# HGRN2 mixer without zero-padded queries: products over a head's 64 rows, results on that parity's partitions, scores and state part in one accumulator

## The chip, the core and the metric

The kernel runs on one core of a Trainium2 chip. The core has five engines that run side by side, each with its own instruction queue, executed in order: TensorE (PE in the rows; its weight loads are shown as PEld), VectorE (DVE), ScalarE (ACT), GpSimd (POOL) and SyncE (SP, which only starts transfers here). An engine waits for another through semaphores. The metric is the device time of one execution in microseconds (us).

## What is computed

One inference step of a two-layer decoder trunk, 512 prompt tokens and 8 single-token samples, 1024 features. Each layer normalises its input, projects it with one matrix, hands the columns to four mixers (A: HGRN2, B: RWKV-7, C: dilated attention, D: pooling), gates them, and projects back. The change is in mixer A, which has 4 heads of 64 features and runs in chunks of 64 tokens:

```python
def step(s, inp):                       # one chunk; q, k, v, log f per head
    G = jnp.cumsum(gb, axis=2)
    o_inter = jnp.einsum('bhtk,bhkv->bhtv', qb * jnp.exp(G), s)
    diff = G[:, :, :, None, :] - G[:, :, None, :, :]
    decay = jnp.where(causal, jnp.exp(jnp.where(causal, diff, 0.0)), 0.0)
    att = jnp.einsum('bhtk,bhsk,bhtsk->bhts', qb, kb, decay)
    o_intra = jnp.einsum('bhts,bhsv->bhtv', att, vb)
    s_new = exp(G_last) * s + einsum('bhsk,bhsv->bhkv', kb * exp(G_last - G), vb)
    return s_new, o_inter + o_intra
```

## The kernel before

Activations lie with features on the 128 partitions and tokens along the free dimension. The 256 features of mixer A are two tiles `th` of 128; each tile holds two heads, one on partitions 0 to 63 and one on 64 to 127 (their parity, `pp`; `ROWS` are the two slices).

The input projection (`project`, tiles `pj`) is the bulk of TensorE's work: every operand is split in two exact parts (`hh`, `hl` for the input, `whi`, `wlo` for the weights; POOL makes `wlo`, ACT `whi`), and three matmuls of 256 or 264 columns are made per product. The class `Flow` writes TensorE's program in one order: it takes steps of the mixers' generators (`stream_A`, `stream_B`, ...), whose `yield cost, latency` says how long a step is thought to keep TensorE and how long the next one has to wait for other engines, and lays steps of the projections between them. A scheduler then moves instructions within limits. Since each engine runs in order, a TensorE instruction that waits for DVE holds up every projection behind it.

`stream_A` per layer: the queries `aq` are copied into `aqz`, which has for each chunk and head the query in that head's 64 rows and zeros in the other 64 (two tiles, one per `th`). `adg` holds products of keys and queries of the same token (the diagonal of the scores `aatt`). `sample_values` and the loop behind it handle the 8 samples. `to_tokens` turns the values by transposes on TensorE (`tok`, then `avtm`, 128 tokens on the partitions). Then six levels follow, for blocks of 1, 2, ..., 32 tokens: at each, `alv` holds the products of the keys in the left halves with the queries in the right halves of every pair of blocks, DVE writes them into the scores where a mask says so (line 727), and queries, keys and the block decays (`atot`) are scaled for the next level (lines 731 to 739); the queries of parity 0 on DVE, those of parity 1 on POOL. Behind the levels come the samples' read (`srd`), the keys turned (`aktm`), the state products of all chunks (`akv`), the states `aS` by a chain on DVE, and the outputs: `ao` within the chunks and `aos` from the states before them, in two PSUM tiles, added by DVE.

In `alv` a matmul has the 64 keys of a chunk over all 128 rows as its stationary operand and both heads' padded queries as 64 columns:

```python
mm(p[ROWS[c % 2], x:x + 64].rearrange("p (a n b) -> p a n b", a=2, b=b),
   k[:, th, 64 * c:64 * c + 64],
   qz[th][:, c].rearrange("p a (n w b) -> p a n w b", w=2, b=b)[:, :, :, 1, :])
```

A matmul with fp32 operands stands in the trace as two records. The size in a record (`128*64`) is the rows and columns of the stationary operand; a result on partitions 0 to 63 or 64 to 127 uses the left or right half of the array's columns, operands on one half of the partitions use one half of its rows. `stream_B` runs beside A; in this text its tiles `sBt`, `sBa` (samples' state), `bZ`, `bA`, `bMB` (products of a chunk), `bT` (an inverse by substitution on DVE), `bX`, `bXT`, `bU`, `bS` appear.

## Time and profile before

| | |
|---|---|
| median of 3 runs | 782.69 us (782.3 to 784.27) |
| profiled execution, first to last instruction (span) | 781.0 us |
| TensorE busy | 715.5 us (92%) |
| VectorE busy | 593.2 us (76%) |
| GpSimd busy | 384.7 us (49%) |
| ScalarE busy | 365.2 us (47%) |

The profile tells of the profiled execution only its span; the median of the runs lies 1.7 us above it. Busy time is the union of an engine's instructions. TensorE's records overlap and their ends are modelled, so its share tells where it waits rather than how fast it works.

### The profile page before, as it was taken

The page shows a single profiled execution, that of the slowest core. Times are in us where ns is not written, and L with a number is a line of the kernel's source. Part 1 is how long each engine was busy: PE and PEld are TensorE (multiplying, and loading weights), DVE is VectorE, ACT ScalarE, POOL GpSimd, SP SyncE. Part 2 cuts the span into 40 slices and gives each one's busy share as a digit, 9 for nine tenths or more (in the row PEclk, how much of TensorE's full clock was granted, in tenths as well). Part 3 has the DMA queues.
Part 4 walks back from the last instruction along what each step waited for, and adds up shares of the span by engine and source line. Part 5 has one row for each costly group of instructions (what it writes and reads, how often), then busy time and mean ns, then how long its engine had stood idle before and what let it go on. Part 6 is the DMA issues. An engine that isn't in the chain of part 4 may idle for free. (4 is left out here: it accounts for less than half of the span.)

```text
span 781.0 us, 18348 instructions
## 1 busy us (share of the span) xinstructions
PE 715.5 (92%) x7297; PEld 626.3 (80%) x7297; DVE 593.2 (76%) x1263; ACT 365.2 (47%) x778; POOL 384.7 (49%) x348
## 2 busy tenths in 40 slices
PE   2999989698789999999998999879889999999998
PEld 1687769487779998787888989768778989777898
DVE  4558759999998465788747897986999765587873
ACT  5233667014243465674235688412233547477520
POOL 2335427874753243236637756686554332223662
PEclk9999999897899999999998999899889999999999
DMA  9979755152232155337263323515232134135222
GB/s 330 351 276 335 226 168 153 41 163 69 82 98 56 40 183 192 125 97 272 69 190 96 118 68 98 147 56 150 69 95 86 56 99 150 56 113 163 98 77 102
DMA packets 67446, 105.74 MB, mean 135 GB/s; under 512 B 18336, under 2 KB 26848, under 8 KB 67360
## 3 DMA queue, kind: packets, MB, share of 16 engines
q1 hardware_dynamic: 67216, 104.50, 41.8%
q8 instruction: 57, 0.93, 0.5%
q14 instruction: 29, 0.24, 0.1%
q10 hardware_dynamic: 144, 0.06, 0.0%
HBM read 88.20 MB, written 14.22 MB: 131 GB/s over the span
## 5 line engine op out<-in xcount | busy, mean ns | idle before, releaser
L237 POOL TENSOR_TENSOR wlo<-wraw,whi 128x512 fp32r<-128x512 f32 x144 | 203.1, 1416 | 235.4 <-ACT whi L261 203.8
L269 PE MATMUL pj<-hh,whi 128*128 128x256 f32 (+1 forms) x928 | 278.0, 308 | 17.9 <-DVE raw L632 6.9
L269 PE MATMUL pj<-hl,whi 128*128 128x256 f32 (+1 forms) x928 | 268.3, 296 | 0.6 <-DVE hl L254 0.6
L269 PE MATMUL pj<-hh,wlo 128*128 128x264 f32 (+1 forms) x896 | 262.2, 298 | 0.5 <-POOL wlo L237 0.5
L269 PEld LDWEIGHTS pj<-hh,whi 128*128 128x128 f32 x928 | 182.3, 200 | 36.1 <-issue 12.6
L269 PEld LDWEIGHTS pj<-hl,whi 128*128 128x128 f32 x928 | 183.1, 200 | 4.6 <-issue 2.7
L269 PEld LDWEIGHTS pj<-hh,wlo 128*128 128x128 f32 x896 | 176.3, 199 | 6.2 <-issue 4.1
L261 ACT ACTIVATE whi<-wraw 128x512 fp32r<-128x512 f32 (+1 forms) x146 | 90.6, 623 | 161.5 <-PE pj L269 128.6
L269 PE MATMUL pj<-ml,whi 128*128 128x264 f32 (+1 forms) x256 | 72.5, 286 | 2.0 <-DVE cst L250 1.4
L269 PE MATMUL pj<-mh,whi 128*128 128x256 f32 (+1 forms) x256 | 72.6, 291 | 0.3 <-ACT mh L261 0.3
L269 PE MATMUL pj<-mh,wlo 128*128 128x256 f32 (+1 forms) x256 | 71.5, 283 | 0.0
L237 POOL TENSOR_TENSOR gate<-gate,raw 128x520 f32<-128x520 f32 x16 | 22.1, 1383 | 69.9 <-ACT gate L258 34.3
L254 DVE SCALAR_TENSOR_TENSOR x<-pj,mod,x 128x256 f32<-128x256 f32 x64 | 30.8, 481 | 33.1 <-PE pj L269 32.7
L269 PEld LDWEIGHTS pj<-mh,whi 128*128 128x128 f32 x256 | 47.4, 188 | 4.8 <-issue 2.6
L269 PEld LDWEIGHTS pj<-ml,whi 128*128 128x128 f32 x256 | 48.2, 188 | 3.3 <-DVE ml L237 2.7
L269 PEld LDWEIGHTS pj<-mh,wlo 128*128 128x128 f32 x256 | 48.0, 188 | 0.6 <-POOL wlo L237 0.4
L269 PE MATMUL ada<-adaw,sc 128*32 128x256 f32 (+1 forms) x448 | 33.9, 375 | 11.9 <-DVE nacc L237 11.8
L269 PEld LDWEIGHTS ada<-adaw,sc 128*32 128x32 f32 x448 | 12.4, 115 | 20.6 <-DVE nacc L237 11.8
L269 PE MATMUL alv<-aqz,ak 128*64 128x64 f32 x384 | 20.6, 249 | 6.6 <-DVE ak L237 6.6
L254 DVE SCALAR_TENSOR_TENSOR bX<-bX,bfac,bS 64x64 f32<-64x64 f32 x56 | 15.6, 279 | 14.2 <-PE bS L269 12.8
L269 PEld LDWEIGHTS alv<-aqz,ak 128*64 128x64 f32 x384 | 17.2, 157 | 10.0 <-issue 4.5
L1123 DVE COPY bUV<-bU 64x128 f32<-64x128 f32 x16 | 4.7, 295 | 23.3 <-ACT bUV L261 23.1
(409 smaller groups left out, 1456.1 us busy)
## 6 DMA issues: line engine op xcount, KB each, us to landing
wraw<-in_w_in_dram SPq DMA_DIRECT2D x112, 256.0 KB, 2.8
adaw<-in_ada_w_dram SPq DMA_DIRECT2D x48, 512.0 KB, 5.5
wraw<-in_w_out_dram SPq DMA_DIRECT2D x32, 256.0 KB, 2.8
x<-in_x_dram SPq DMA_DIRECT2D x8, 520.0 KB, 5.8
ckT<-in_ckT_dram SPq DMA_DIRECT2D x8, 320.0 KB, 3.2
x<-xmid SPq DMA_DIRECT2D x4, 520.0 KB, 5.8
cvr<-in_cvr_dram SPq DMA_DIRECT2D x4, 512.0 KB, 5.3
xmid<-x SPq DMA_DIRECT2D x7, 260.0 KB, 2.0
```

The lines of the kernel that those rows point to most:

```text
L237: return eng.tensor_tensor(out=out, in0=a, in1=b, op=op)
L254: return V.scalar_tensor_tensor(out=out, in0=a, scalar=s, in1=b, op0=op0, op1=op1)
L261: return A.activation(out, a, AF.Copy)
L269: return PE.matmul(out, lhsT, rhs, start=start, stop=stop)
L1123: V.tensor_copy(UV[ROWS[1], 1], pv[ROWS[1]])
```

## The change

The padded queries are gone: `aq` itself is scaled in place, and every product of mixer A takes one head's 64 rows on both sides, with the result on the same 64 partitions. `to_rows` takes the place of `to_tokens` for keys and values (a product with a piece of the identity instead of a transpose). A level makes 32 matmuls of 32 columns instead of 16 of 64, and the masked copy into the scores stands behind the scaling for the next level. The scaling of the queries is done on DVE over 128 partitions, POOL has none of it. Scores and state part go into one accumulator, so the copies and sums behind `ao` become one copy per half. The costs and latencies in the `yield`s are other numbers too. Comments are removed throughout, which moves line numbers by two at most outside `stream_A`.

```diff
@@ -660,39 +660,49 @@
             ts(k, k, omlb[:, l, j:j + 1], ALU.mult)
         return use
 
+    def to_rows(dst, src):
+
+        for hf in range(2):
+            p = mm_ps("rows")
+            for c in range(4 * hf, 4 * hf + 4):
+                for th in range(2):
+                    i = 64 * (2 * (c % 4) + th)
+                    for pp, r in enumerate(ROWS):
+                        mm(p[r, i:i + 64], src[r, th, 64 * c:64 * c + 64], ident[r, 64 * pp:64 * pp + 64])
+            copy(dst[:, 8 * hf:8 * hf + 8, :], p.rearrange("p (i d) -> p i d", d=64))
+            yield 800.0, 700.0 * hf
+
     def stream_A(l, L, flow):
+
         yield "aq1"
         yield 0.0, 3500.0
         q = L.t["aq"]
         att = f1k("aatt").rearrange("p (a t) -> p a t", t=64)
-        # each chunk's queries, per head with zeros in the other head's rows
-        qz = [f1k("aqz").rearrange("p (c a t) -> p c a t", a=2, t=64) for _ in range(2)]
-        for th in range(2):
-            G.memset(qz[th], 0.0)
-            for pp, r in enumerate(ROWS):
-                copy(qz[th][r, :, pp, :], q[r, th, PR].rearrange("p (c t) -> p c t", t=64))
         zq = sample_queries(q[:, :, SM])
-        yield 0.0, 2500.0
+        yield 0.0, 1000.0
         yield "af1"
         f, k = L.t["af"], L.t["ak"]
+
+        def chunk(x, r, c, th):
+            return x[r, th, 64 * c:64 * c + 64]
 
         for hf in range(2):
             p = mm_ps("adg")
             for c in range(4 * hf, 4 * hf + 4):
                 for th in range(2):
-                    i = 128 * (2 * (c // 2 % 2) + th)
-                    mm(p[ROWS[c % 2], i:i + 128].rearrange("p (a t) -> p a t", a=2),
-                       k[:, th, 64 * c:64 * c + 64], qz[th][:, c])
+                    i = 64 * (2 * (c % 4) + th)
+                    for r in ROWS:
+                        mm(p[r, i:i + 64], chunk(k, r, c, th), chunk(q, r, c, th))
             mul(att[:, 8 * hf:8 * hf + 8, :], p.rearrange("p (a t) -> p a t", t=64),
                 bc(C["eye64"][:, None, :], [128, 8, 64]))
-            yield 1100.0, 200.0
+            yield 800.0, 200.0
         yield "ai1"
         v = L.tile("av")
         yield 0.0, 700.0
         vbs = sample_values(v, svs[l, "A"])
-        vtm = f1k("avtm").rearrange("p (c n) -> p c n", c=4)
-        yield from to_tokens(vtm, v)
-        # the samples' step reads q, f and k as they come
+        vtm = f1k("avtm").rearrange("p (i d) -> p i d", d=64)
+        yield from to_rows(vtm, v)
+
         S0s = []
         for i in range(2):
             S0 = h512("sA0")
@@ -708,79 +718,67 @@
             load(O["A_s"][l, i], S0)
             yield 0.0, 1500.0
         for th in range(2):
-            for pp, r in enumerate(ROWS):
-                x = qz[th][r, :, pp, :]
-                mul(x, x, f[r, th, PR].rearrange("p (c t) -> p c t", t=64))
-        yield 0.0, 2500.0
+            mul(q[:, th, PR], q[:, th, PR], f[:, th, PR])
+        yield 0.0, 2000.0
         tot = f[:, :, PR]
         for i in range(6):
             b = 1 << i
             p = mm_ps("alv")
             for c in range(8):
                 for th in range(2):
-                    x = 64 * (2 * (c // 2) + th)
-                    mm(p[ROWS[c % 2], x:x + 64].rearrange("p (a n b) -> p a n b", a=2, b=b),
-                       k[:, th, 64 * c:64 * c + 64],
-                       qz[th][:, c].rearrange("p a (n w b) -> p a n w b", w=2, b=b)[:, :, :, 1, :])
-            dst = att.rearrange("p a (n w b) -> p a n w b", w=2, b=b)[:, :, :, 1, :]
-            m = bc(C["mright"][:, None, i, :], [128, 16, 32]).rearrange("p a (n b) -> p a n b", b=b)
-            V.copy_predicated(dst, m, p.rearrange("p (a n b) -> p a n b", a=16, b=b))
+                    x = 32 * (2 * c + th)
+                    for r in ROWS:
+                        mm(p[r, x:x + 32].rearrange("p (n b) -> p n b", b=b), chunk(k, r, c, th),
+                           chunk(q, r, c, th).rearrange("p (n w b) -> p n w b", w=2, b=b)[:, :, 1, :])
             nblk = TP // (2 * b)
             tw = tot.rearrange("p j (n w) -> p j n w", w=2)
-            kl = k[:, :, PR].rearrange("p j (n w b) -> p j n w b", w=2, b=b)[:, :, :, 0, :]
-            for j in range(2):
-                for pp, r in enumerate(ROWS):
-                    x = qz[j][r, :, pp, :].rearrange("p c (n w b) -> p c n w b", w=2, b=b)[:, :, :, 1, :]
-                    y = tw[r, j, :, 0].rearrange("p (c n) -> p c n", c=8)
-                    mul(x, x, bc(y[:, :, :, None], [64, 8, nblk // 8, b]), eng=(V, G)[pp])
-                mul(kl[:, j], kl[:, j], bc(tw[:, j, :, 1][:, :, None], [128, nblk, b]))
+            for x, w in ((q, 1), (k, 0)):
+                x = x[:, :, PR].rearrange("p j (n w b) -> p j n w b", w=2, b=b)[:, :, :, w, :]
+                for j in range(2):
+                    mul(x[:, j], x[:, j], bc(tw[:, j, :, 1 - w][:, :, None], [128, nblk, b]))
             nt_ = h512("atot")[:, 0:2 * nblk].rearrange("p (j n) -> p j n", j=2) if i == 0 else \
                 stile([128, 2, nblk], f"atot{i}", 1)
             mul(nt_, tw[:, :, :, 0], tw[:, :, :, 1])
             tot = nt_
-            yield 1400.0, 3000.0
+            dst = att.rearrange("p a (n w b) -> p a n w b", w=2, b=b)[:, :, :, 1, :]
+            m = bc(C["mright"][:, None, i, :], [128, 16, 32]).rearrange("p a (n b) -> p a n b", b=b)
+            V.copy_predicated(dst, m, p.rearrange("p (a n b) -> p a n b", a=16, b=b))
+            yield 1450.0, 2500.0
         o_s = sample_read(S0s, zq)
         yield 800.0, 0.0
-        ktm = f1k("aktm").rearrange("p (c n) -> p c n", c=4)
-        yield from to_tokens(ktm, k)
+        ktm = f1k("aktm").rearrange("p (i d) -> p i d", d=64)
+        yield from to_rows(ktm, k)
         S = f1k("aS").rearrange("p (t c v) -> p t c v", t=2, c=8)
         p = [mm_ps("akv") for _ in range(2)]
         for c in range(8):
             for th in range(2):
-                for pp, r in enumerate(ROWS):
-                    x, y = 64 * (4 * th + c // 2), 128 * th + 64 * pp
-                    mm(p[c % 2][r, x:x + 64], ktm[ROWS[c % 2], c // 2, y:y + 64], vtm[ROWS[c % 2], c // 2, y:y + 64])
+                x = 64 * (2 * (c % 4) + th)
+                for r in ROWS:
+                    mm(p[c // 4][r, x:x + 64], ktm[r, 2 * c + th, :], vtm[r, 2 * c + th, :])
         for c in range(8):
             for th in range(2):
-                x = p[c % 2][:, 64 * (4 * th + c // 2):64 * (4 * th + c // 2) + 64]
+                x = 64 * (2 * (c % 4) + th)
+                x = p[c // 4][:, x:x + 64]
                 if c:
                     stt(S[:, th, c, :], S[:, th, c - 1, :], tot[:, th, c:c + 1], x, ALU.mult, ALU.add)
                 else:
                     V.tensor_copy(S[:, th, 0, :], x)
-        yield 2600.0, 0.0
+        yield 1450.0, 0.0
         load(O["A_p"][l], S[:, :, 7, :])
         yield 0.0, 2000.0
         o, sq = fmix("ao"), fm("asq")
-        for cp in range(2):
-            # within the chunks, and from the states before them
-            p, pS = mm_ps("ao"), mm_ps("aos")
-            for c2 in range(4):
-                c = 2 * c2 + cp
-                for th in range(2):
-                    for pp, r in enumerate(ROWS):
-                        i, y = 64 * (2 * c2 + th), 128 * th + 64 * pp
-                        mm(p[r, i:i + 64], vtm[ROWS[cp], c2, y:y + 64], att[ROWS[cp], 4 * c2 + 2 * th + pp, :])
-                        if c:
-                            mm(pS[r, i:i + 64], S[r, th, c - 1, :], qz[th][r, c, pp, :])
-            dst = o[:, :, PR].rearrange("p a (c w t) -> p a c w t", w=2, t=64)[:, :, :, cp, :]
-            p4, s4 = (x.rearrange("p (c a t) -> p a c t", c=4, a=2) for x in (p, pS))
-            if cp == 0:
-                copy(dst[:, :, 0], p4[:, :, 0])
-            c0 = 1 - cp
+        for hf in range(2):
+
+            p = mm_ps("ao")
             for th in range(2):
-                copy(dst[:, th, c0:], p4[:, th, c0:])
-                add(dst[:, th, c0:], s4[:, th, c0:], dst[:, th, c0:])
-            yield 2500.0, 0.0
+                for c in range(4 * hf, 4 * hf + 4):
+                    i = 256 * th + 64 * (c % 4)
+                    for r in ROWS:
+                        mm(p[r, i:i + 64], vtm[r, 2 * c + th, :], att[r, 2 * c + th, :], True, c == 0)
+                    for r in ROWS if c else ():
+                        mm(p[r, i:i + 64], S[r, th, c - 1, :], chunk(q, r, c, th), False, True)
+            copy(o[:, :, 256 * hf:256 * hf + 256], p.rearrange("p (a t) -> p a t", a=2))
+            yield 1500.0, 0.0
         act(sq[:, :, PR], o[:, :, PR], AF.Square)
         V.tensor_copy(o[:, :, SM], o_s)
         act(sq[:, :, SM], o_s, AF.Square)
```

The places below are from the programs of before and of the change, one engine at a time, in the order in which the engine executes them.

On VectorE, in the first layer behind the diagonal of the scores (`aatt<-adg`), the queries are multiplied by the decays. Before:

```order
L237 TENSOR_TENSOR sBt<-sBa,ba 128x4x64 [waits PE_50]
L237 TENSOR_TENSOR sBt<-sBa,ba 128x4x64
L237 TENSOR_TENSOR aatt<-adg,c_eye_638 128x512 [waits PE_50]
L237 TENSOR_TENSOR aqz<-aqz,af 64x8x64 [waits PE_50,Activation_50]
L237 TENSOR_TENSOR aatt<-adg,c_eye_638 128x512 [waits PE_50]
L237 TENSOR_TENSOR aqz<-aqz,af 64x8x64 [waits Activation_50] x3
L237 TENSOR_TENSOR bMB_1855<-bA,c_mb 128x256 [waits PE_50]
```

The same place in the change:

```order
L237 TENSOR_TENSOR bZ_1705<-br,bE 64x4x64
L237 TENSOR_TENSOR sBt<-sBa,ba 128x4x64 [waits PE_50]
L237 TENSOR_TENSOR sBt<-sBa,ba 128x4x64 [waits DVE_50]
L237 TENSOR_TENSOR aq<-aq,af 128x512 [waits PE_50]
L237 TENSOR_TENSOR aatt<-adg,c_eye_638 128x512 [waits PE_50]
L237 TENSOR_TENSOR aq<-aq,af 128x512
L512 COPY av<-pj_1687 128x264 [waits PE_50]
```

Four products of 64 partitions have become two of 128, and products of B (`bZ`), which stood ahead of these rows with other work between, now stand right ahead of them.

On VectorE at the second level of the first layer, behind that level's `alv`. Before:

```order
L237 TENSOR_TENSOR aqz<-aqz,atot 64x8x16x2 [waits PE_50]
L727 COPY_PREDICATED aatt<-c_mright,alv 128x256x2 [waits PE_50]
L237 TENSOR_TENSOR ak<-ak,atot 128x128x2
L237 TENSOR_TENSOR aqz<-aqz,atot 64x8x16x2
L237 TENSOR_TENSOR ak<-ak,atot 128x128x2
L1015 STREAM_TRANSPOSE bXT<-bX 128x512 [waits DMAHW0_50,DVE_50]
```

In the change:

```order
L237 TENSOR_TENSOR aq<-aq,atot 128x128x2 [waits PE_50]
L237 TENSOR_TENSOR ak<-ak,atot 128x128x2
L237 TENSOR_TENSOR ck<-ck,csqk 128x2x520 [waits DVE_50,Pool_50]
L237 TENSOR_TENSOR aq<-aq,atot 128x128x2 [waits PE_50]
L237 TENSOR_TENSOR ak<-ak,atot 128x128x2
L745 COPY_PREDICATED aatt<-c_mright,alv 128x256x2
```

VectorE has as many products per level as before, over twice the partitions, and the masked copy has moved behind them; the two that POOL had (`aqz`, parity 1) are in neither list.

On TensorE in the first layer, behind a step of B (`bU`), the outputs of A begin. Before:

```order
L269 MATMUL bU<-bR,bXF 64x64 x3
L269 MATMUL ao<-aatt,avtm 64x64 x5
L269 MATMUL aos<-aqz,aS 64x64 [waits PE_50]
L269 MATMUL ao<-aatt,avtm 64x64
L269 MATMUL aos<-aqz,aS 64x64
L269 MATMUL ao<-aatt,avtm 64x64
```

In the change:

```order
L269 MATMUL bU<-bR,bXF 64x64 x3
L269 MATMUL ao<-aatt,avtm 64x64 x4
L269 MATMUL ao<-aq,aS 64x64 x2
L269 MATMUL ao<-aatt,avtm 64x64 x2
L269 MATMUL ao<-aq,aS 64x64 x2
```

The state part goes into `ao` itself, two matmuls (one per parity) at a time.

## Rows read from the trace of the kernel before

**Rows 1.** The page, part 1: busy time, share and instructions of each engine.

```profile
PE 715.5 (92%) x7297; PEld 626.3 (80%) x7297; DVE 593.2 (76%) x1263; ACT 365.2 (47%) x778; POOL 384.7 (49%) x348
```

**Rows 2.** Busy time by stretch; its columns are in the first line.

```profile
core 0: us, PE busy (x) PEld busy (x) DVE busy (x) ACT busy (x) POOL busy (x), PEclk, DMA share, GB/s
...
140.00:155.00 15.00, 10.26 (x62) 7.45 (x62) 14.43 (x23) 0.63 (x1) 12.18 (x13) 0.77 0.12 35
155.00:187.00 32.00, 29.97 (x285) 26.57 (x283) 30.32 (x59) 8.53 (x17) 19.63 (x19) 0.96 0.40 117
187.00:232.00 45.00, 37.69 (x605) 34.49 (x605) 44.44 (x73) 14.65 (x31) 27.85 (x24) 0.80 0.31 92
232.00:290.00 58.00, 57.72 (x842) 52.41 (x842) 37.34 (x86) 29.46 (x65) 21.29 (x17) 1.00 0.30 86
493.00:526.00 33.00, 26.20 (x169) 22.89 (x170) 30.55 (x42) 6.98 (x13) 24.75 (x22) 0.84 0.36 109
526.00:550.00 24.00, 24.00 (x249) 21.48 (x247) 16.33 (x26) 7.81 (x15) 17.32 (x18) 1.00 0.47 142
550.00:620.00 70.00, 62.04 (x967) 57.39 (x967) 67.51 (x134) 25.22 (x50) 33.89 (x32) 0.90 0.25 75
```

**Rows 3.** TensorE's waits, 98 to 232 us: total us, times, longest.

```profile
PE sBa L269 <- DVE sBt L237: 7.0, 2, 4.7
PE alv L269 <- DVE ak L237: 3.9, 3, 3.2
...
PE pj L269 <- DVE raw L632: 3.5, 4, 2.4
```

**Rows 4.** VectorE's longest wait for another engine, 140 to 232 us.

```profile
DVE aatt L237 <- PE adg L269: 0.5, 1, 0.5
```

**Rows 5.** Timeline of TensorE: start, length in us, of bursts of records.

```profile
155.21 1.04 PE L559 MATMUL tok<-c_ident,av 128*128 128x128 f32 x8
...
158.59 1.96 PE L269 MATMUL bA<-bZ,ba 64*64 64x128 f32 x32
...
233.98 1.20 PE L269 MATMUL bZ<-bX,bMB 32*32 32x32 f32 x64
...
236.03 1.20 PE L269 MATMUL alv<-aqz,ak 128*64 128x64 f32 x32
...
248.76 1.84 PE L269 MATMUL srd<-sz,sA 128*128 128x4 f32 x16
...
255.00 0.45 PE L269 MATMUL bU<-bR,bXF 64*64 64x64 f32 x8
...
265.45 1.17 PE L269 MATMUL akv<-avtm,aktm 64*64 64x64 f32 x63
```

**Rows 6.** The same view: the outputs' first burst, first and last of 56 records.

```profile
278.05 0.27 PE L269 MATMUL ao<-aatt,avtm 64*64 64x64 f32 x1
...
279.68 0.28 PE L269 MATMUL aos<-aqz,aS 64*64 64x64 f32 x3
```

**Rows 7.** VectorE's groups: busy us, mean ns of one, idle before.

```profile
L237 DVE TENSOR_TENSOR aqz<-aqz,atot 64x256 f32<-64x256 f32 x20 | 18.1, 906 | 0.2
...
L237 DVE TENSOR_TENSOR ak<-ak,atot 128x256 f32<-128x256 f32 x20 | 10.9, 547 | 0.0
...
L237 DVE TENSOR_TENSOR aqz<-aqz,af 64x512 f32<-64x512 f32 (+1 forms) x12 | 10.1, 843 | 0.4 <-PE adg L269 0.2
```

**Rows 8.** Timeline of VectorE and of POOL at the first two levels.

```profile
197.46 0.41 DVE L237 TENSOR_TENSOR aqz<-aqz,af 64x256 f32<-64x256 f32 x1
...
202.74 0.92 DVE L237 TENSOR_TENSOR aqz<-aqz,atot 64x256 f32<-64x256 f32 x1
...
201.94 2.33 POOL L237 TENSOR_TENSOR aqz<-aqz,atot 64x256 f32<-64x256 f32 x2
```

**Rows 9.** The tile aqz on POOL: count, min/median/max ns, first and last start.

```profile
L671 POOL MEMSET aqz<- x4: 947/952/954, 124.6 to 488.2; 128x1024 f32 x4
```

## The prediction

> **What bounds the kernel now.** I read the page first: TensorE is busy 92% of the span, VectorE 76%, GpSimd 49% [rows 1]. That makes TensorE the first suspect, but the share is a mean over stages, so I then read busy time by stretch [rows 2]. There are two kinds of stretch. In 232 to 290 and 526 to 550 us TensorE is busy throughout at a granted clock of 1.00 (2.4 GHz): here every nanosecond added to TensorE is paid. In 140 to 187 and 187 to 232 us, and in the second layer in 493 to 526 and 550 to 620 us, VectorE is the one that is (almost) always busy: 44.44 of 45 us, 67.51 of 70. TensorE idles there: 4.7 + 2.0 + 7.3 us up to 232, 6.8 in 493 to 526, 8.0 in 550 to 620, and the clock column shows stretches at the lower level (1.2 GHz): 0.77, 0.80, 0.84, 0.90 on average. The waits say the same from both sides. In 98 to 232 us TensorE waits longest for VectorE: `sBa` for `sBt`, the levels' `alv` for scaled keys, a projection for a copy out of PSUM [rows 3]; VectorE's own longest wait for another engine in 140 to 232 us is 0.5 us [rows 4]. The reader is to see that mixer A's levels lie in the stretches that VectorE bounds, and its tail (`tok`, `akv`, `ao`) in those that TensorE bounds.
>
> **The price of a small matmul.** The change makes all of A's products 64 rows by 64 columns, alternating between two opposite quarters of the array. What a record of that kind costs is read from bursts [rows 5]; a burst's spacing is its length less the 0.2 to 0.3 us that one record lasts, over the count less one. `alv` before (all rows, two column halves in turn): (1.20 − 0.22)/31 = 32 ns. `akv` before visits all four quarters: (1.17 − 0.22)/62 = 15 ns. `bU` visits two opposite quarters, the new pattern, with the same 64 columns: (0.45 − 0.22)/7 = 33 ns; `bA`, the same pattern with 128 columns, 54 ns, of which half is 27. So two quarters in turn cost about 30 ns a record, and the new pattern leaves half of the array empty where `akv` filled it.
>
> One price has no row: 64 stationary columns with only 32 streamed, which is the new level. Below: `bZ`, two quarters with 32 stationary and 32 streamed columns, 16 ns. Above: `bU`, 33 ns. The choice follows from `srd`: it streams 4 columns past 128 stationary ones and still takes (1.84 − 0.25)/15 = 106 ns, as long as `tok` with 128 streamed, (1.04 − 0.27)/7 = 110 ns. The wider of the two operands sets the price, so I take 30 ns, near the upper end.
>
> **TensorE's account, both layers, at full clock.** Levels: 12 × (64 × 30 − 32 × 32 ns) = 12 × (1.92 − 1.02) = +10.8 us (bounds 0 and +13). `to_rows` against `to_tokens`, keys and values: 4 × (64 × 30 ns − 8 × 110 ns) = 4 × 1.04 = +4.2. `akv`: 2 × (1.92 − 64 × 15 ns) = +1.9. `adg`: before 32 records of 128 columns at `bA`'s 54 ns, 1.74 us; after 64 at 30, 1.92: +0.4. `ao` with `aos`: before 56 records between 278.05 and 279.73 us [rows 6], 31 ns each, and as many after at 30: nothing. Sum +17.3 us (bounds +6.5 and +21), in a change that removes zeros.
>
> A rule of the Trainium skill is weighed here, since it speaks against the change harder than this sum. The row first: `bA` and `bU` send the two row halves in turn into one and the same PSUM tile, and take 54 ns for 128 columns where one record of `tok`, with as many streamed columns over the whole array, takes 110: the halves overlap [rows 5]. The page "TensorEngine Tiling (Array Packing)", section "Restrictions and Gotchas", says that different row tiles cannot access the same PSUM bank at the same time. By it the new pairs would take turns, 60 ns a record, and the account would be some +63 us; the trace does not bear it out.
>
> **What of it is on the path.** Paid in full, because TensorE bounds the stretch: the keys' `to_rows` (2 × 1.04 = 2.1), `akv` (1.9), the second layer's values (1.0), the first layer's last level, which lies behind 232 us (0.9), and half of two levels of the second layer in 550 to 620 us, where both engines are near full (0.9): +6.8 us. The other 10.5 us lie where TensorE waits for VectorE, and are covered by the 14.0 + 6.8 + 8.0 us of idle time there; without that cover they would be paid as well.
>
> **VectorE's account.** Queries times decays: before eight products of 64x512 in the group of 10.1 us; four small ones of 0.41 us [rows 8] taken off leave 8.5 us, and after the change four of the same length per partition do it: −4.2 us [rows 7]. Levels: VectorE keeps as many products, but POOL's part is gone. The DVE products on `aqz` take 906 ns on average, those on `ak`, with the same number of elements per partition, 547 [rows 7]; and the same product took 0.41 us alone and 0.92 us while POOL worked on its pair [rows 8]. At the price of `ak` the 20 would take 7.2 us less. The bounds are nothing (other POOL work moves into the gap) and 7.2; I take three quarters, 5.4, since POOL's splitting of weights stays and only the pair is gone. Sum −9.6 us, all of it in stretches that VectorE bounds, so it counts in full. The zeroing on POOL (4 × 0.95 us [rows 9]), ACT's copies of the queries, the copies and sums behind `ao` and the eight products fewer cost the path nothing now and give nothing: those engines are not waited for there, or TensorE is the bound. The masked copy behind the scaling lets the next level's keys be ready earlier, which is worth nothing while VectorE's queue is full. With `sBt` and `bZ` moved, TensorE's wait for `sBa` should shrink and one before `bA` appear: the work on VectorE is the same.
>
> **Sum.** 781.0 − 9.6 + 6.8 = 778.2 us span; with the 1.7 us by which the median lies above the span, 779.9 us, 0.4% under the median of 782.69. A measurement of this kernel can tell about 0.3%, 2.35 us, from no change.
>
> **Rivals.** *TensorE takes over the bound in the level stretches* (slower). For it: in 187 to 232 us it idles only 7.3 us, at a clock of 0.80, where added records can cost up to double; four levels add 3.6 us warm and up to 7.2 cold, and VectorE's relief takes another 3 to 4 out of the same idle time. Against it: fewer waits mean more time at the upper clock. It decides from the point where added work and relief together exceed 7.3 us there (8.0 in 550 to 620). If half of the covered 10.5 us comes out and half of the relief is lost: 782.7 + 6.8 + 5.2 − 4.8 = 789.9 us.
>
> *Gain and loss cancel* (no change). POOL's weight splits slide into the gaps and VectorE's levels stay at half their relief: 782.7 + 6.8 − 6 = 783.5 us.
>
> *The 64x32 records are cheap* (faster). If they cost `bZ`'s 16 ns, the levels add nothing, exposed work falls by 1.8 us, and more cover is left: 778 us, and about 775 with the levels' full relief. Against it stands `srd`.
>
> *The row halves take turns in a PSUM bank.* That is a mechanism in which each pair takes 60 ns a record; of +63 us some 29 would be covered: 782.7 + 63 − 29 = about 817 us. `bA` and `bU` speak against it. It is what the page named above would make of the change.
>
> **Chances.** Forecast 0.36, cancelling 0.25, TensorE the bound 0.28, cheap records 0.09, turns in a bank 0.02. Faster by over 0.3%: 0.45; within: 0.25; slower: 0.30. The range has to hold cases of both signs: it goes from 770 us (cheap records, the relief at its bound, and a stall or two fewer) to 791 us (TensorE the bound) and leaves the bank case and the ends of the order's shuffling out. The forecast's own range is 775 to 780.5 us.
>
> **What would show it.** Right: `alv` bursts of 64 records in about 1.9 us at full clock, `rows` and `akv` bursts of 64 in about 1.9 us; VectorE's `aq<-aq,atot` near 0.5 to 0.6 us; VectorE still without waits in 140 to 232 us, that stretch shorter by some 5 us; 232 us and later longer by 2 to 4 us per layer. Wrong: `alv` bursts near 1.0 us (price), new VectorE waits for `alv` (TensorE is the bound), unchanged `aq` products (no relief), or waits of TensorE that are as long as before in spite of fuller bursts.

## The result and the profile after

The changed kernel takes 815.07 us (median of 4 runs, 812.04 to 815.91) against 783.48 us (4 runs) of the kernel before: slower by 31.6 us between these two medians. The ratio on record is 1.0363, 95% interval 1.0325 to 1.0400, which makes it 28.5 us; the shares of the loss below go by the ratios, since the kernel before lay up to 3 us higher beside the experiments. Executions that ran more than 1.5% above the fastest of the same kernel (one each of before_new_costs, pool_pair and late_levels) are left out of medians and ratios. The forecast was 779.9 us, the range 770 to 791. The profiled execution has a span of 810.3 us, 29.3 above the 781.0 of before.

Part 1 of the changed kernel's page, beside [rows 1]:

```profile
PE 734.4 (91%) x7969; PEld 646.2 (80%) x7969; DVE 574.9 (71%) x1251; ACT 359.3 (44%) x764; POOL 361.7 (45%) x320
```

TensorE is busy 18.9 us longer, near the +17.3 of the forecast's account. VectorE works 18.3 us less. The span grew all the same, by TensorE's 18.9 us and by 10.4 us more in which TensorE is idle. Where: the busy time by stretch, cut at the end of the first layer (the start of the last record of `ms<-ntail` there), first of the kernel before, then of the changed one:

```profile
0.00:417.42 417.42, 378.72 (x3884) 321.20 (x3884) 311.62 (x680) 191.52 (x407) 194.97 (x171) 0.96 0.52 168
417.42:781.00 363.58, 336.79 (x3415) 305.10 (x3413) 281.58 (x583) 173.65 (x372) 189.68 (x178) 0.95 0.32 98
```

```profile
0.00:427.58 427.58, 386.35 (x4219) 329.56 (x4220) 301.47 (x674) 188.71 (x400) 179.22 (x157) 0.95 0.50 164
427.58:810.30 382.72, 348.01 (x3751) 316.61 (x3749) 273.42 (x577) 170.55 (x365) 182.53 (x164) 0.94 0.31 93
```

The reader is to see that the first layer is 10.2 us longer (7.6 of TensorE's busy time, 2.5 idle) and the second 19.1 (11.2 and 7.9). VectorE's busy time falls by 10.2 and 8.2 us and neither layer is shorter for it.

The stretches of [rows 2] in the changed kernel, at the same times of its own span:

```profile
140.00:155.00 15.00, 11.72 (x150) 10.15 (x147) 14.93 (x23) 2.49 (x4) 13.10 (x14) 0.95 0.07 19
155.00:187.00 32.00, 31.44 (x301) 28.13 (x301) 22.99 (x49) 6.67 (x13) 18.19 (x19) 0.89 0.40 125
187.00:232.00 45.00, 36.48 (x776) 33.66 (x777) 43.91 (x75) 15.43 (x33) 21.17 (x16) 0.92 0.29 85
526.00:550.00 24.00, 17.65 (x199) 15.96 (x201) 13.34 (x25) 3.74 (x7) 16.45 (x17) 0.86 0.45 140
550.00:620.00 70.00, 60.39 (x966) 56.25 (x963) 62.59 (x120) 19.88 (x40) 27.79 (x22) 0.85 0.25 75
```

VectorE was busy in 30.32 of the 32 us of 155 to 187; now in 22.99. It did not pass the relief on: it waits. Its waits for other engines in 140 to 232 us (total, times, longest), beside the 0.5 us of [rows 4]:

```profile
DVE bMB L237 <- PE bA L269: 7.8, 4, 4.4
```

And TensorE's waits over the whole span:

```profile
PE pj L269 <- DVE raw L632: 8.9, 6, 3.8
PE alv L269 <- DVE ak L237: 8.9, 6, 2.7
PE svT L577 <- DVE svc L575: 6.7, 2, 6.3
```

So each of the two engines now waits for the other in the same stretches. `alv` waited 6.6 us in the kernel before, `raw` 6.9, and `svT` had no long wait.

The price of the new records, from the timeline of TensorE, beside [rows 5]:

```profile
220.27 1.94 PE L269 MATMUL alv<-aq,ak 64*64 64x32 f32 x60
260.99 1.10 PE L269 MATMUL rows<-c_ident,ak 64*64 64x64 f32 x32
263.58 1.96 PE L269 MATMUL akv<-avtm,aktm 64*64 64x64 f32 x58
```

(1.94 − 0.22)/59 = 29 ns for a level's record, 27 and 30 for the others: the 30 ns of the forecast, and no dearer for 64 streamed columns than for 32. The row halves do not take turns: a pair of records that write the two halves of one PSUM tile lasts 58 ns, where the prediction's rival had 120. The Trainium skill's page "TensorEngine Tiling (Array Packing)", section "Restrictions and Gotchas", says that different row tiles cannot access the same PSUM bank simultaneously; the trace differs, as `bU` had said.

VectorE's groups (busy us, mean ns of one), beside [rows 7]:

```profile
L237 DVE TENSOR_TENSOR aq<-aq,atot 128x256 f32<-128x256 f32 x20 | 14.5, 723 | 0.1
L237 DVE TENSOR_TENSOR ak<-ak,atot 128x256 f32<-128x256 f32 x20 | 12.7, 633 | 0.0
L237 DVE TENSOR_TENSOR aq<-aq,af 128x512 f32<-128x512 f32 x4 | 3.2, 802 | 0.0
L237 DVE TENSOR_TENSOR aq<-aq,af 128x256 f32<-128x256 f32 x4 | 1.7, 416 | 0.0
```

The level products took 3.6 us less (18.1 to 14.5) where the forecast had 5.4, and the keys' products 1.8 more (10.9 to 12.7): without its own pair GpSimd does other work beside them. The query times decay products fell from 10.1 to 4.9 us. Together −7.0 us where the forecast had −9.6.

### The profile page after: what moved, and what is told of

The parts are those of the page before. It is cut to its first block, busy times and chain, and to the rows that moved or that the text cites. A ratio compares the mean times of both kernels' runs of the same rounds, so it can differ in the third digit from the quotient of the medians.

```text
span 810.3 us, 19571 instructions
## 1 busy us (share of the span) xinstructions
PE 734.4 (91%) x7969; PEld 646.2 (80%) x7969; DVE 574.9 (71%) x1251; ACT 359.3 (44%) x764; POOL 361.7 (45%) x320
## 5 line engine op out<-in xcount | busy, mean ns | idle before, releaser
L269 PE MATMUL pj<-hh,whi 128*128 128x256 f32 (+1 forms) x928 | 274.7, 305 | 20.2 <-DVE raw L632 8.9
L269 PE MATMUL pj<-ml,whi 128*128 128x256 f32 (+1 forms) x256 | 72.5, 285 | 0.6 <-DVE ml L237 0.6
L254 DVE SCALAR_TENSOR_TENSOR x<-pj,mod,x 128x256 f32<-128x256 f32 x64 | 30.8, 483 | 41.5 <-PE pj L269 39.8
L269 PE MATMUL alv<-aq,ak 64*64 64x32 f32 x768 | 30.8, 235 | 8.9 <-DVE ak L237 8.9
L269 PEld LDWEIGHTS alv<-aq,ak 64*64 64x64 f32 x768 | 28.5, 153 | 11.9 <-DVE ak L237 7.2
L269 PEld LDWEIGHTS ada<-adaw,sc 128*32 128x32 f32 x448 | 12.3, 114 | 20.5 <-DVE nacc L237 12.0
L1226 DVE CUSTOM_DVE_ANT_0 cS<-cs,c_atab 128x128 f32<-128x128 f32 (+3 forms) x32 | 15.1, 488 | 15.3 <-PE cs L269 15.2
```

The lines of the kernel that those rows point to most:

```text
L254: return V.scalar_tensor_tensor(out=out, in0=a, scalar=s, in1=b, op0=op0, op1=op1)
L269: return PE.matmul(out, lhsT, rhs, start=start, stop=stop)
L1226: V.tensor_tensor_reduce(out=s, in0=p[:, 0:w], in1=C["atab"][:, 384 - 128 * i:512], scale=1.0, scalar=-3e38, op0=ALU.add, op1=ALU.max, acc ...
```

## The experiments

Theory 1 was that the added records are paid in full, wherever they lie, and that VectorE's relief is worth nothing. Theory 2 was that the loss comes from the order of TensorE's queue: the diff also changes the two numbers that each step of mixer A yields (its cost, which sets how many projections are put behind it, and its latency, which holds its next step back). All ratios are to the kernel before, run beside the experiment, where it lay at 784.3 to 786.6 us.

| kernel | median us | ratio (95%) | first, second layer us |
|---|---|---|---|
| before, profiled | 783.48 | 1 | 417.4, 363.6 |
| changed | 815.07 | 1.0363 (1.0325 to 1.0400) | 427.6, 382.7 |
| old_costs | 797.87 | 1.0151 (1.0110 to 1.0193) | 425.4, 370.5 |
| before_new_costs | 813.15 | 1.0394 (1.0347 to 1.0440) | 442.8, 380.1 |
| before_twice | 797.28 | 1.0143 (1.0106 to 1.0181) | 425.4, 370.0 |
| pool_pair | 814.27 | 1.0373 (1.0328 to 1.0418) | 427.6, 387.1 |
| four_quarters | 819.71 | 1.0435 (1.0394 to 1.0476) | 430.4, 390.0 |
| four_with_old_costs | 795.92 | 1.0135 (1.0102 to 1.0167) | 418.7, 375.0 |
| tail_costs | 813.59 | 1.0359 (1.0332 to 1.0387) | 423.5, 384.4 |
| level_costs | 812.12 | 1.0342 (1.0306 to 1.0379) | 428.7, 385.0 |
| first_costs | 819.70 | 1.0436 (1.0403 to 1.0469) | 434.3, 382.6 |
| late_levels | 798.64 | 1.0179 (1.0137 to 1.0220) | 415.1, 378.9 |
| svc_act | 796.04 | 1.0153 (1.0130 to 1.0176) | 426.4, 371.5 |
| svt_late | 815.25 | 1.0385 (1.0346 to 1.0424) | 425.7, 385.3 |
| four_svt_late | 794.58 | 1.0134 (1.0092 to 1.0177) | 418.4, 378.1 |
| before_levels_new | 812.50 | 1.0342 (1.0298 to 1.0386) | 429.8, 381.6 |
| before_first_new | 800.48 | 1.0200 (1.0151 to 1.0249) | 425.9, 376.8 |
| before_late0 | 788.16 | 1.0042 (1.0017 to 1.0067) | 421.2, 364.9 |
| four_late0 | 795.92 | 1.0149 (1.0113 to 1.0185) | 417.5, 379.4 |

The lengths of the layers are those of the one profiled execution, cut at the same record as above. Two profiled executions of four_quarters differ by 0.1 us in the first layer and 3.2 us in the second, so differences of a few us between second layers tell little. The profiled execution of before_new_costs took 824.7 us, 11.5 above its median; no reading below rests on it.

**The numbers alone.** old_costs undoes them (in the diff: behind the queries, diagonals, rows, ahead of the levels, a level, states, outputs), before_new_costs puts them into the old layout:

```diff
-        yield 0.0, 1000.0
+        yield 0.0, 2500.0
-            yield 800.0, 200.0
+            yield 1100.0, 200.0
-            yield 800.0, 700.0 * hf
+            yield 430.0, 700.0 * hf
-        yield 0.0, 2000.0
+        yield 0.0, 2500.0
-            yield 1450.0, 2500.0
+            yield 1400.0, 3000.0
-        yield 1450.0, 0.0
+        yield 2600.0, 0.0
-            yield 1500.0, 0.0
+            yield 2500.0, 0.0
```

> The changed kernel with the costs and latencies that mixer A's steps tell the order of TensorE set back to the numbers of the kernel before; the work is the same. Theory 1 (TensorE pays for the added records wherever they lie): 810 to 820 us, as the changed kernel's 815. Theory 2 (the new order's waits are what was lost, above all the 6.6 us before svT in the second layer and the longer waits for copies): 785 to 800 us.

> The kernel before, unchanged in its work, with the costs and latencies of the changed kernel in mixer A's steps. Theory 1 (the numbers alone cost what old_costs gave back, some 17 us, whatever the records are): 796 to 803 us. Rival (the old layout does not mind them, they hurt only with the new records): 783 to 788 us.

The old numbers give the changed kernel 2.1% back, 16.6 of the 28.5 us (17.2 between the medians); the new ones make the kernel before as slow as the changed one, with not a record more. Theory 2 holds for more than half of the loss. In before_new_costs and in before_first_new (below) the number behind `to_tokens` changes for mixer C's values too, since C calls the same helper; in the changed kernel C keeps 430. before_levels_new, which sets the two numbers of mixer A's levels and nothing else, costs 3.4% by itself, so the finding does not hang on that. Its stretches by layer, and those of old_costs:

```profile
0.00:429.80 429.80, 382.88 (x3883) 323.63 (x3884) 304.27 (x680) 191.59 (x407) 197.38 (x171) 0.94 0.50 163
429.80:811.40 381.60, 342.15 (x3415) 309.20 (x3413) 283.24 (x583) 174.38 (x372) 194.85 (x178) 0.94 0.30 93
```

```profile
0.00:425.41 425.41, 382.45 (x4220) 327.25 (x4220) 306.42 (x674) 188.71 (x400) 181.32 (x157) 0.95 0.51 165
425.41:795.90 370.49, 342.28 (x3751) 312.12 (x3749) 274.66 (x577) 170.99 (x365) 183.30 (x164) 0.95 0.31 96
```

In before_levels_new the same records as in the kernel before keep TensorE busy 9.5 us longer, at a mean granted clock of 0.94 (0.96 and 0.95 before), and it is idle 20.8 us more: an order with more waits costs twice, in the waits and in the stretches at 1.2 GHz (100.0 us of the span, 69.5 in the kernel before). In old_costs the records of the changed kernel keep it busy only 9.2 us longer than the kernel before (724.7 against 715.5 us), against 18.9 in the changed kernel: the total holds the projections at the lower clock too, and does not give the price of the records.

**TensorE's work alone.** before_twice leaves the old layout and numbers as they are:

```diff
-                    mm(p[ROWS[c % 2], x:x + 64].rearrange("p (a n b) -> p a n b", a=2, b=b),
+                    for _ in range(2):
+                        mm(p[ROWS[c % 2], x:x + 64].rearrange("p (a n b) -> p a n b", a=2, b=b),
```

> The kernel before with every product of the levels issued twice into the same place: 384 records of 32 ns more, 12.3 us of TensorE work at full clock, in the level stretches alone; VectorE's work is the same. Theory 1 (the idle time there covers nothing, since TensorE has enough else to do and the waits stay): 783.5 + 12 = 793 to 798 us. Rival (the forecast's cover: VectorE bounds these stretches): 783 to 787 us.

```profile
0.00:425.40 425.40, 385.62 (x4076) 330.39 (x4076) 311.77 (x680) 191.58 (x407) 193.98 (x171) 0.95 0.51 165
425.40:795.40 370.00, 342.24 (x3607) 310.46 (x3605) 282.28 (x583) 172.91 (x372) 193.69 (x178) 0.96 0.32 96
```

TensorE is busy 12.3 us longer, and the kernel takes 1.43% or 11.2 us longer (the span 14.4). That the 12.3 equals 384 records at 32 ns is an accident. Each record is followed by its own repetition, on the same half of the array's columns: at a granted clock of 1.00 that took 37 ns a record (second line below), where the halves in turn took 32. And several bursts ran mostly at 1.2 GHz (first line, granted clock 0.53):

```profile
202.65 4.05 PE L269 MATMUL alv<-aqz,ak 128*64 128x64 f32 x60
227.79 2.42 PE L269 MATMUL alv<-aqz,ak 128*64 128x64 f32 x60 [0.89 <-DVE ak L237]
```

The group of the levels' records grew by 21.2 us, first before, then before_twice:

```profile
L269 PE MATMUL alv<-aqz,ak 128*64 128x64 f32 x384 | 20.6, 249 | 6.6 <-DVE ak L237 6.6
L269 PE MATMUL alv<-aqz,ak 128*64 128x64 f32 x768 | 41.8, 257 | 7.4 <-DVE ak L237 7.2 <-DVE bT L1008 0.2
```

while the projections' records were busy 8 us less (504.0 to 496.0). The idle time of some 29 us in these stretches did not hide all of the added work, as the forecast would have it; how much of the 21.2 us it hid cannot be told. The order is not quite the same either: the third and fourth levels of the first layer stand behind 871 and 886 projections instead of 839 and 866. VectorE's waits in 140 to 232 us show a part of where the time went:

```profile
DVE aqz L237 <- PE alv L269: 2.4, 1, 2.4
```

VectorE now waits for the level's products, and TensorE's idle time is still there afterwards (39.8 and 27.8 us by layer, 38.7 and 26.8 before).

**VectorE's relief.** pool_pair hands the second parity's query products back to GpSimd:

```diff
-                    mul(x[:, j], x[:, j], bc(tw[:, j, :, 1 - w][:, :, None], [128, nblk, b]))
+                    for pp, r in enumerate(ROWS) if w else [(0, slice(0, 128))]:
+                        mul(x[r, j], x[r, j], bc(tw[r, j, :, 1 - w][:, :, None], [128 // (1 + w), nblk, b]),
+                            eng=(V, G)[pp])
```

> The changed kernel with half of the levels' query products (the second parity's rows) back on GpSimd, as before the change: VectorE gets its slow pairs back, some 7 us of busy time, TensorE's work is the same. Theory 1: VectorE's relief was worth little, so 813 to 820 us. Rival (the relief counts in full on the path, and was eaten by something larger): 821 to 828 us.

No change of the time, with VectorE busy 5.4 us longer and GpSimd 17.6. The group that was to be slowed keeps its mean:

```profile
L237 DVE TENSOR_TENSOR aq<-aq,atot 64x256 f32<-64x256 f32 x20 | 14.6, 730 | 0.5 <-PE alv L269 0.3
```

With the pair on GpSimd or without it, the mean is the same in this order: other work of GpSimd takes the pair's place. This was run with the new numbers only, and gives back 5.4 of VectorE's 18.3 us.

**The records' price taken off.** four_quarters sends the odd chunks' products to the other parity's partitions (values, keys and scores alike, so that the result stays the same), each kind into two PSUM tiles; four_with_old_costs does the same with the old numbers. Both make one step of the two for the rows and for the diagonals, add VectorE work (two masked copies for one, an addition of the outputs), and four_quarters has numbers of its own, not those of the changed kernel: 1000 for the rows, the diagonals, a level (1450 in the change) and the states (1450).

```diff
-                    for r in ROWS:
-                        mm(p[r, x:x + 32].rearrange("p (n b) -> p n b", b=b), chunk(k, r, c, th),
+                    for pp, r in enumerate(ROWS):
+                        mm(p[c % 2][ROWS[pp ^ c % 2], x:x + 32].rearrange("p (n b) -> p n b", b=b), chunk(k, r, c, th),
```

> The changed kernel with the odd chunks' products sent to the other parity's partitions, so that A's small products visit all four quarters of the array, in two PSUM tiles each; the masked copies become two of half the size, and the odd chunks' sums of values get an accumulator and an addition of their own. Theory 1: a record falls from 29 to about 15 ns in all but the state part, some 17 us less on TensorE in both layers, and all of it comes out: 795 to 801 us; about 785 if VectorE's relief then shows too. Theory 2 (order and waits alone): 810 to 820 us.

> The four-quarter kernel with its steps' costs raised to those that the kernel before gave the same steps (levels 1400 and 3000, tail 2600 and 2500). Theory 1 (in an order that leaves the levels as far apart as before, TensorE's work is paid in full, so the 15 us that the four quarters take off A's records come out): 781 to 787 us. Rival (the records are hidden whatever the order, and what is left of the loss has another cause): 794 to 800 us.

A level's 64 records do take 1.16 us now, 15 ns each (timeline of four_with_old_costs), and the `alv` group 18.4 us in place of 31.0:

```profile
225.21 1.16 PE L269 MATMUL alv<-aq,ak 64*64 64x32 f32 x64
```

With its own numbers four_quarters gains nothing (one more execution took 819.1 us), but its order is another one, so this says little of the records. With the old numbers TensorE is busy 11.9 us less than in old_costs, but the time is 2 us less, inside the two intervals. The rival of each expectation came true in the total. By layer it is not one thing:

```profile
0.00:418.71 418.71, 377.66 (x4220) 321.99 (x4220) 304.15 (x682) 188.68 (x400) 182.51 (x157) 0.95 0.51 168
418.71:793.70 374.99, 335.12 (x3751) 302.90 (x3749) 271.55 (x585) 170.61 (x365) 182.35 (x164) 0.94 0.30 95
```

The first layer, where the levels stand at the same places of the order as in old_costs, ends 6.7 us earlier (418.7 against 425.4; 417.4 in the kernel before). The second has 7.2 us less work of TensorE and is 4.5 us longer, with 39.9 us of idle time against 28.2. The 4.5 us are little above the 3.2 by which two executions of one kernel differed.

**One number or all.** Three runs set back one group of numbers each in the changed kernel, two put one group into the kernel before.

> The changed kernel with only the costs of the tail's steps (states 1450 to 2600, outputs 1500 to 2500 each) set back. Theory 1 (what the numbers lose is lost behind mixer A's tail, where mixer B's chain is left with too few projections between its steps): 799 to 806 us. Rival (the levels' numbers are what counts): 812 to 818 us.

> The changed kernel with only the levels' two numbers set back (cost 1450 to 1400, latency 2500 to 3000); in the first layer 219 instead of 193 projection matmuls stand between the first and the last level again. Theory 1 (the levels' distance is the most of what the numbers lose): 798 to 806 us. Rival (the steps ahead of the levels are what counts): 811 to 818 us.

> The changed kernel with only the numbers of the steps ahead of the levels set back (2500 after the queries, 1100 for the diagonals, 430 for the rows); the levels stay as close together as in the changed kernel. Theory 1 (the levels' distance counts): 808 to 816 us. Rival (the early steps count): 797 to 804 us.

> The kernel before with the levels' two numbers of the changed kernel alone (1450 and 2500). Theory (the levels' distance from one another is what counts): 796 to 812 us, the first layer's end moving from 417 to some 425 to 435 us. Rival (only all numbers together do it): 783 to 788 us.

> The kernel before with the changed kernel's numbers in the steps ahead of the levels alone; the first layer's levels stand where they stood. Theory (the levels' distance counts): 783 to 790 us. Rival (any other order than the one the numbers were found with costs some 10 us or more): 794 to 805 us.

No group alone mends the changed kernel. In the kernel before the levels' two numbers cost 28 us by themselves and the early steps' numbers 16; they do not add up to the 31 us of all. What the levels' numbers do can be counted in the program: the projection matmuls that TensorE's queue holds ahead of the first record of each of the six levels, counted from each layer's start, and how many lie between the first and the last.

```
kernel               layer 1                          layer 2                         between
before               761 800 839 866 935  981         758 797 827 863  910  998       220 240
changed              761 801 829 868 881  954         752 785 806 839  864  896       193 144
old_costs            761 800 839 881 935  981         758 797 827 857  919 1001       220 243
before_new_costs     761 799 836 872 887  954         752 785 816 862  904  920       193 168
before_levels_new    761 799 836 872 887  954         758 793 823 859  909  958       193 200
before_first_new     761 800 839 872 935  981         752 791 815 862  906  953       220 201
four_with_old_costs  761 800 839 881 935  981         767 800 833 863  920  974       220 207
svt_late             761 800 839 881 935  981         809 845 881 908  941  992       220 183
late_levels          761 812 870 935 980 1084         758 809 854 905 1038 1087       323 329
before_late0         761 812 862 935 981 1084         758 797 827 863  910 1007       323 249
```

Over all the kernels of this study, those not in the list too, the second layer takes 363.6 to 371.5 us in every order with 240 to 249 projections between its levels, and 375.0 to 390.0 in every one with 144 to 210, or 329, whatever the records are. It is a pattern, not yet a cause: the first layer keeps to it only roughly.

**More distance.** late_levels raises the levels' latency from 3000 to 4500 on top of the old numbers; before_late0 and four_late0 do so in the first layer alone.

> The changed kernel with all the old costs and the levels' latency raised further, from 3000 to 4500: the last level stands behind 1084 projection matmuls in place of 981. Theory 1 (TensorE's work and not its waits is what is left above the kernel before): 795 to 805 us, no gain. Rival (the levels are still too close for VectorE): 785 to 793 us.

> The kernel before with a longer latency of the levels (4500 for 3000) in the first layer alone. With the new layout the first layer ended 10 us earlier with that number (415.1 against 425.4 us in late_levels and old_costs). Theory (the first layer's levels are too close for VectorE in the old order too): 773 to 780 us. Rival (the kernel before stands at an order that any step away makes worse): 787 to 800 us.

> The four-quarter kernel with the old costs and the same longer latency in the first layer. Theory (order and records add up in the first layer): first layer 409 to 412 us, 786 to 791 us in all. Rival (the first layer is at its end with 415 us, or the second layer's order loses it again): 794 to 800 us.

The first layer of late_levels is the shortest of all, 415.1 us, and its second loses 8 us. Put into the kernel before, the same step makes the first layer longer (421.2) and the kernel 0.4% slower. No gain carried over from one layout to the other. The first layers of late_levels and of before_late0, with the levels at nearly the same places:

```profile
0.00:415.10 415.10, 378.53 (x4219) 325.87 (x4220) 301.09 (x674) 189.58 (x400) 180.06 (x157) 0.96 0.51 169
0.00:421.20 421.20, 379.08 (x3883) 322.81 (x3884) 304.95 (x680) 192.08 (x407) 192.58 (x171) 0.94 0.51 166
```

Here the changed layout ends its first layer 6.1 us ahead of the old one, although it has 336 records more. The four quarters take nothing off it in this order either (four_late0 417.5 us). So the records are not paid wherever they lie, as Theory 1 has it: it depends on the order.

**The wait at svT.** In the second layer of the changed kernel TensorE stands 6.35 us. Its timeline, and VectorE's for the same time:

```profile
534.33 0.38 PE L577 MATMUL svT<-c_ident,svc 128*16 128x128 f32 x1 [6.35 <-DVE svc L575]
```

```profile
526.03 4.30 DVE L237 TENSOR_TENSOR bZ<-br,bE 64x256 f32<-64x256 f32 x4
532.15 1.41 DVE L237 TENSOR_TENSOR sBt<-sBa,ba 128x256 f32<-128x256 f32 x4
533.48 0.42 DVE L512 COPY av<-pj 128x264 f32<-128x264 f32 x1
533.94 0.34 DVE L575 COPY svc<-av 128x16 f32<-128x16 f32 x1
```

svc_act makes the copy on ScalarE (`V.tensor_copy(c, ...)` becomes `copy(c, ...)`); svt_late and four_svt_late raise the latency ahead of it from 700 to 5000, in the second layer. All three stand on the old numbers (old_costs or four_with_old_costs), where the wait was 6.8 us; the helper of svc_act serves mixer B too.

> The changed kernel with the old costs, and the copy of the samples' values ahead of svT (0.34 us) on ScalarE in place of VectorE, where it stands behind 8 us of other work in the second layer. Theory 1 (the 6.6 us wait at svT is paid in full): 790 to 793 us. Rival (the wait moves to the next operation that needs VectorE): 796 to 800 us.

> The changed kernel with the old costs, and in the second layer alone the steps behind the values' projection (svT and the rows) held back by a latency of 5000 in place of 700, so that 38 more projection matmuls stand ahead of svT; the first layer's order is the same row for row. Theory (the 7 us wait at svT is projections put too late, and paid in full): 790 to 793 us. Rival (another wait takes its place, since VectorE's queue is what it waits for): 795 to 800 us.

> The four-quarter kernel with the old costs and the same later svT in the second layer. Its first layer already ended as early as that of the kernel before (418.7 against 417.4 us); the second had 11 us more of waits than old_costs. Theory (with the wait at svT gone the fewer records count in the second layer too): 784 to 790 us. Rival (new waits in the second layer): 793 to 799 us.

The wait stayed at 6.1 us in svc_act, now for a ScalarE copy that waits for `av`, the projection's own evacuation, which is what stands deep in VectorE's queue. In svt_late it moved: a projection waits for `av`, and later steps wait longer.

```profile
PE pj L269 <- DVE av L512: 6.7, 1, 6.7
PE cT L1242 <- DVE cS L250: 6.3, 3, 3.5
PE alv L269 <- DVE ak L237: 5.4, 2, 5.0
```

An edit that only put one step later, with the first layer's queue unchanged, cost some 18 us against old_costs by the ratios; four_svt_late took as long as four_with_old_costs. None of the versions beats the kernel before.

## Why the prediction was wrong, by its steps

**The price of a record: right.** 30 ns forecast, 27 to 30 measured. That TensorE's busy time rose by 18.9 us where the account had +17.3 is in part luck: with the same records it rose by 9.2 in old_costs, since fewer projections fell into stretches at 1.2 GHz there (152 of 3520 records, 206 in the kernel before, 194 in the changed one).

**"Covered by the 14.0 + 6.8 + 8.0 us of idle time": the first step that failed.** In before_twice work added to those stretches alone made the kernel 11.2 us longer, with the idle time still there. The idle time is TensorE waiting for a result of VectorE, and VectorE waits for products of TensorE there (7.8 us for `bA` in the changed kernel, 2.4 for `alv` in before_twice): work that is put ahead of the products can delay the next wait as much as it fills this one. That reading is argued from the waits. In another order (late_levels against before_late0) the first layer is not longer for the added records.

**"Sum −9.6 us, all of it in stretches that VectorE bounds, so it counts in full": the second.** VectorE was busy in 140 to 232 us but not the bound by itself. Its busy time fell by 18.3 us over the span, new waits of 7.8 us for `bA` took up part of it, and pool_pair, which gives 5.4 us back to VectorE, shows no price. The size was off too: −7.0, since GpSimd's weight splits moved beside the level products (last section).

**The order: the step that was missing, and the largest.** The diff's new costs and latencies had no term in the sum; the prediction said that it "leaves ... the ends of the order's shuffling out" of the range. They cost 16.6 us of the 28.5 (old_costs, by the ratios), and 31 in the old layout. "TensorE's wait for `sBa` should shrink and one before `bA` appear" was right for the first layer (7.0 to 2.2 us, and 1.4 us), and others took their place: `raw`, `alv` and `svT`.

**What is left, 1.5% or some 12 us (old_costs).** Its cause stays open. For the records: the prediction's own sum with nothing covered and no relief is +17.3; both layers of old_costs stand within 0.5 us of before_twice, which has added TensorE work alone; and in the first layer, with the levels at equal places of the order, the four quarters take 6.7 of 8.0 us off. Against: with the levels later the new layout's first layer is shorter than the old one's, and the four quarters take nothing off. In the second layer the four quarters gave nothing, in another order. Two parts of the change were never run by themselves: the masked copy behind the scaling, and the single accumulator.

**The rivals.** "TensorE takes over the bound" (789.9 us, chance 0.28) is the nearest: added work that comes out in the level stretches is what before_twice shows, at 797.3. It has no term for the order either. The turns in a bank (817 us) hit the time by accident; the bursts refute them. Cheap records are refuted too. The cancelling rival's −6 is not the sum of its own terms (4.2 + half of 5.4 is 6.9), which changes nothing here.

**Left open:** why just some 240 projections between the levels of the second layer serve, and whether a search over the numbers would bring the four quarters below the kernel before; at the old numbers they stand at 1.0135.

## What to carry to other kernels

Where a program's order comes from a table of costs or yields, and a diff changes those with the work, run the kernel before with the new numbers first: here that alone gave the changed kernel's time. Idle time of an in-order engine need not be cover: see whether what it waits for waits for that engine itself. Issuing existing records twice tests it, if one looks at what the repeated records really took and whether the order stayed. Two engines that wait for each other have no single bound, so relief on one is not to be counted in full.

## What the runs showed of the hardware

A VectorE product of 128x256 takes 0.41 us alone and took 1.2 to 1.5 us beside a weight split of GpSimd, which works on other tiles altogether. Timeline of the changed kernel, GpSimd and VectorE:

```profile
211.22 1.81 POOL L237 TENSOR_TENSOR wlo<-wraw,whi 128x512 fp32r<-128x512 f32 x1
```

```profile
211.84 1.48 DVE L237 TENSOR_TENSOR aq<-aq,atot 128x256 f32<-128x256 f32 x1
218.94 0.41 DVE L237 TENSOR_TENSOR aq<-aq,atot 128x256 f32<-128x256 f32 x1
```

The slow one ends 0.28 us after the split (213.32 against 213.03 us), and so do the other three `aq` products of the levels that began during a split: they look as if they had waited for the whole of it.

And the price of a small record with 64 stationary columns went by how many quarters are visited in turn, not by whether it streams 32 or 64 columns: 27 to 30 ns at two quarters with either, 15 ns at four with 32. With 128 streamed columns two quarters take 54 ns (`bA`).
